# First loop of a fused transformer layer: every shift vector as a VectorE dot product, scale and shift weights in their own buffers, the first token tile in halves, a sixth pair of split weights

## The chip, the core and the metric

The kernel runs on one core of a Trainium2 chip. The engines named here are TensorE (PE in the profile, its weight loads PEld), VectorE (DVE), ScalarE (ACT), GpSimd (POOL) and SyncE (SP), whose queue issues the loads from device memory. The metric is the device time of one launch in microseconds (us); smaller is better.

## The reference

One layer over 512 latent tokens and 256 context tokens of width 1024: a half-step SwiGLU feed-forward block, a token-mixing block (latent attention beside a chunked gating MLP), and a second feed-forward block, each with a modulated RMS norm ahead of it. The change concerns the first norm and the first feed-forward weights only:

```python
mx = jnp.split((jax.nn.silu(c) @ w_ada + b_ada)[:, None, :], N_MOD, axis=-1)
mc = jnp.split((jax.nn.silu(c_ctx) @ w_ada + b_ada)[None, None, :], N_MOD, axis=-1)
...
def modulate(h, shift, scale):
    return h * (1 + scale) + shift
def ffn_sublayer(h_in, shift, scale, gate, norm_w, w1, w3, w2):
    h = modulate(rms_norm(h_in, norm_w), shift, scale)
    return h_in + 0.5 * gate * swiglu(h, w1, w3, w2)
x = ffn_sublayer(x, mx[0], mx[1], mx[2], norm1_w, ffn1_w1, ffn1_w3, ffn1_w2)
ctx = ffn_sublayer(ctx, mc[0], mc[1], mc[2], norm1_w, ffn1_w1, ffn1_w3, ffn1_w2)
```

`mx` belongs to the latent tokens, `mc` to the context tokens. Shift and scale of the first block are 2 x 1024 numbers each, and each of them is a dot product of 1024 terms with a column of `w_ada`.

## The kernel before, in words

Features lie on the 128 partitions, tokens along the free axis. The width of 1024 is cut into 8 tiles `k`; `x` holds 8 x 768 numbers per partition, two groups of 256 latent and 128 context tokens each. Every matrix product is made exact enough by splitting both operands into a high and a low part (`hh`/`hl` for activations, the `oph`/`opl` pair for weights) and adding three matmuls: high x high, high x low, low x high (`mm3`, and `first_mm` in the first loop). A pair comes from `st.pair()`; there are `OPS` = 5 of them, reused in turn. Making a pair is one ScalarE copy (`oph`) and one VectorE subtraction (`opl`).

All VectorE, ScalarE and GpSimd instructions of the part looked at here are kept in the order in which the program text has them (`nc.ordered`), and so are the TensorE instructions passed to `pin`. A helper records them, so nearly all VectorE and ScalarE rows have line 60. Loads on SP are placed by the scheduler of the framework, in the order in which it finds them ready.

**Start (lines 253 to 507).** `x` is loaded in four pieces, then the weights of the first tiles. ScalarE and VectorE square `x` (`square0`, 4 buffers, tag `sqx0`); TensorE sums the squares over the partitions by a matmul with `ones` (line 487) into `sumx`; `rstd_start` and `rstd_end` turn the sum into 1/rms by a table root on ScalarE (`r`) and one Newton step of three VectorE instructions (`v`). TensorE also multiplies `sc` (silu of the two conditioning vectors) by the identity, which spreads it over all partitions in `cb`.

**First loop (lines 530 to 575),** over `k`. It multiplies the 8 tiles of the normed latent tokens by the weights of the first two feed-forward tiles (`NFIRST` = 2, two matrices each, so 4 PSUM banks `pbs`), and makes the operands of the next tile meanwhile:

- *Scale and shift of tile k+2.* `ada_row` multiplies `sc` by the weights on TensorE (line 318); the result is a row of 2 x 128 numbers, which `ada_copy` (ScalarE) copies and `ada_col` (line 330) turns into a column by a tiny matmul; a ScalarE instruction makes the factor `a` from it. The shift comes either out of the same row (tiles in `ROWS2` = 1, 2, 3, whose row has 256 columns) or, for the other tiles, from two VectorE dot products over 1024 numbers (`ada_dot`, output `junk`, one for latent, one for context tokens), which `ada_shift` issues.
- *Operands of tile k+1.* `first_x` (VectorE, output `hfull`) is x times `a` times 1/rms; `first_h` (ScalarE, `hh`) adds the shift `s` and rounds to the high part; `first_l` (VectorE, `hl`) makes the low part.
- *Matmuls of tile k* (line 525), 12 of 512 columns: `first_mm` for 2 of the 4 banks, then the column of tile k+1, the row of tile k+2, and the other 2 banks.
- *Context tokens.* Their squares (ScalarE) and the sum of the squares (VectorE) come at k = 1 and 2, the sum over partitions at k = 3 (line 538, placed ahead of the column of tile 4), then their normed tiles two at a time, and their matmuls (`first_ctx`, line 518, 24 of 256 columns for two tiles) from k = 4 on.

One load of 1 MB (`block`) brings the scale and the shift weights of a tile, one of 256 KB (`raw`, three buffers) its feed-forward weights. Behind the loop, further feed-forward tiles follow on TensorE in a fixed order (lines 940 to 984).

Of the kernel before, what the change touches and what calls it, by code (L numbers as in the profile page):

```python
# [9 lines left out]
F32 = mybir.dt.float32  # L10
# [3 lines left out]
ALU = mybir.AluOpType  # L14
# [18 lines left out]
NFIRST = 2  # L33
ROWS2 = (1, 2, 3)
W1 = 2 * NFIRST * P
# [139 lines left out]
def layer_kernel(ctx: ExitStack, tc: tile.TileContext, xT, wfirst, wst, wada, wuq, wkpe, cols, wrope, vnw, rope, out):  # L175
# [80 lines left out]
    load_x = lambda k, n, c: nc.sync.dma_start(four(x[:, k : k + n, :], c), four(xT[:, k : k + n, :], c))  # L256
    for k in range(0, NK, 2):
        load_x(k, 2, slice(0, 256))

    def first_units(k):  # L260
        r, rw = st.block(wada, k, sp if k % 3 == 2 else None), st.raw()
        nc.sync.dma_start(rw[:, :W1], wfirst[k])
        return r, rw

    u0, rw0 = st.raw_pool.tile([P, 2048], F32, tag="block", bufs=BLOCKS, name="block_first"), st.raw()
    nc.sync.dma_start(u0[:, :D], wada[0][:, :D])
    nc.sync.dma_start(u0[:, D:], wada[0][:, D:])
    nc.sync.dma_start(rw0[:, :W1], wfirst[0])
    units = [(u0, rw0), first_units(1)]
    units.append(first_units(2))  # L270
    for k in range(0, NK, 4):
# [41 lines left out]

    def ada_row(r, d, kts=range(NK)):
        n = 2 * P if d in ROWS2 else P
        o = pa[0:2, :n]
        for kt in kts:
            pin(nc.tensor.matmul(o, sc[:, kt, :], r[:, kt * n : kt * n + n], start=kt == 0, stop=kt == NK - 1))
        return o

    def ada_copy(o, d):
        n = o.shape[1]
        row = sp.tile([2, 2 * P], F32, tag="row", name=f"row_{d}")[:, :n]
        nc.scalar.copy(row, o)
        return row

    def ada_col(row, d):
        o = [pcol[:, 4 * d + 2 * i : 4 * d + 2 * i + 2] for i in range(2)]
        for i in range(2 if d in ROWS2 else 1):
            pin(nc.tensor.matmul(o[i], row[:, i * P : i * P + P], ident[0:2, 0:2], start=True, stop=True))  # L330
        nc.scalar.activation(
            pairs[0][1][:, d, :], o[0], AF.Identity, bias=b1n[:, d : d + 1], scale=col[:, COL_N1 + d : COL_N1 + d + 1])
        if d in ROWS2:
            nc.scalar.activation(pairs[0][0][:, d, :], o[1], AF.Identity, bias=col[:, d : d + 1])

    def ada_shift(r, d, alone=False):
        for which in range(2) if d not in ROWS2 else ():
            ada_dot(r[:, D:], d, which, accs[:, d, which : which + 1])
            if alone:
                nc.scalar.activation(mod_s[0][which][:, d : d + 1], accs[:, d, which : which + 1], AF.Identity, bias=col[:, d : d + 1])  # L340
            yield
        if not alone and d not in ROWS2:
            nc.scalar.activation(pairs[0][0][:, d, :], accs[:, d, :], AF.Identity, bias=col[:, d : d + 1])

# [93 lines left out]

    def square0(which, k, on_vector=False):
        sel, n, _ = parts[which]  # L440
        sq = sp.tile([P, n], F32, tag=f"sqx{which}", bufs=4 if which == 0 else NK, name=f"sq0_{which}{k}")
        if on_vector:
            nc.vector.tensor_mul(two(sq), sel(x, k), sel(x, k))
        else:
            nc.scalar.activation(two(sq), sel(x, k), AF.Square)
        return sq

    def rstd_start(which, pt):
        n = parts[which][1]
        t = lambda s: sp.tile([P, n], F32, bufs=1, name=f"{s}{which}")  # L450
        r0, v = t("r0"), t("v")
        nc.scalar.activation(r0, pt, AF.Abs_reciprocal_sqrt, bias=epsc, scale=1.0 / D)
        return pt, r0, v

    def rstd_end(pt, r0, v):
# [3 lines left out]
        return v  # L459

    def first_x(k, which):
        sel = parts[which][0]
        nc.vector.scalar_tensor_tensor(sel(hf, k), sel(x, k), mod_a[0][which][:, k : k + 1], two(rs[which]), ALU.mult, ALU.mult)

    def first_h(k, which):
        sel = parts[which][0]
        nc.scalar.activation(sel(hh, k), sel(hf, k), AF.Identity, bias=mod_s[0][which][:, k : k + 1])

    def first_l(k, which):
        sel = parts[which][0]  # L470
        nc.vector.scalar_tensor_tensor(
            sel(hl, k), sel(hf, k), mod_s[0][which][:, k : k + 1], sel(hh, k).bitcast(F32), ALU.add, ALU.subtract)
# [9 lines left out]
    put_cb = lambda w: nc.scalar.copy(cb[:, w, :], bb[w].rearrange("p g c -> p (g c)"))  # L482
    for k in range(0, NK, 2):
        sa = square0(0, k)
        sb = square0(0, k + 1, k in (2, 6))
        nc.vector.tensor_add(sa, sa, sb)
        pin(nc.tensor.matmul(sumx, ones, sa, start=k == 0, stop=k == NK - 2))
# [3 lines left out]
    r0 = rstd_start(0, sumx)  # L491
    row = ada_copy(ada_row(units[0][0], 0), 0)
    shift = ada_shift(units[0][0], 0, True)
    next(shift)
    rs = [rstd_end(*r0)]
    ada_col(row, 0)
    ops = {}

    first_x(0, 0)
    ops[0] = st.operand(units[0][1][:, :W1])  # L500
    first_h(0, 0)
    first_l(0, 0)
    ada_row(units[1][0], 1, range(4))
    put_cb(1)
    for _ in shift:
        pass
    pbs = bigs(4)
    pcs = []

    def first_ctx(k):  # L510
        for i in range(2 * NFIRST):
# [5 lines left out]
            for m, (l, r) in enumerate(((uh, rhs[0]), (uh, rhs[1]), (ul, rhs[0]))):  # L517
                pin(nc.tensor.matmul(o, l[:, c], r, start=k == 0 and m == 0 and w == 0, stop=k == NK - 1 and m == 2,
                                     skip_group_check=True))

    def first_mm(k, i):
        uh, ul = ops[k]
        c = slice(i * P, i * P + P)
        for m, (l, r) in enumerate(((uh, hh), (uh, hl), (ul, hh))):
            pin(nc.tensor.matmul(two(pbs[i]), l[:, c], lat(r, k), start=k == 0 and m == 0, stop=k == NK - 1 and m == 2))

    ctx_h = {3: (0, 1), 4: (2, 3), 5: (4, 5), 6: (6, 7)}
    sqx = {1: 4, 2: 8}
    sqs = []
    for k in range(NK):  # L530
        if k + 3 < NK:
            units.append(first_units(k + 3))
        later = k + 2 < NK
        for i in range(NFIRST):
            first_mm(k, i)
        if k == 3:
            sumx = mm()[:, :256]
            pin(nc.tensor.matmul(sumx, ones, sqs[0], start=True, stop=True))
        if k == 0:
            row = ada_copy(ada_row(units[1][0], 1, range(4, NK)), 1)  # L540
            first_mm(0, NFIRST)
        if k + 1 < NK:
            ada_col(row, k + 1)
        if later:
            o = ada_row(units[k + 2][0], k + 2)
        for i in range(NFIRST + (k == 0), 2 * NFIRST):
            first_mm(k, i)
        shift = ada_shift(units[k + 2][0], k + 2) if later else iter(())
        next(shift, None)
        if k + 1 < NK:  # L550
            first_x(k + 1, 0)
            ops[k + 1] = st.operand(units[k + 1][1][:, :W1])
            first_h(k + 1, 0)
            next(shift, None)
            first_l(k + 1, 0)
        if later:
            row = ada_copy(o, k + 2)
        next(shift, None)
        if k == 3:
            rs.append(rstd_end(*rstd_start(1, sumx)))  # L560
# [6 lines left out]
        for j in ctx_h.get(k - 1, ()):  # L567
            first_ctx(j)
        if k in sqx:
            while len(sqs) < sqx[k]:  # L570
                sqs.append(square0(1, len(sqs)))
                if len(sqs) > 1:
                    nc.vector.tensor_add(sqs[0], sqs[0], sqs[-1])
        if k == 5:
            nc.scalar.activation(epsc2, epsc, AF.Silu)
# [1273 lines left out]
```

## Time and profile before

| | |
|---|---|
| runs | 1157.81, 1159.8, 1160.19 us (median 1159.8) |
| profiled execution | 1158.67 us, its span 1156.8 us |
| TensorE busy over the span | 1138.6 us (98%) |
| VectorE busy | 904.1 us (78%) |
| ScalarE busy | 532.1 us (46%) |
| TensorE clock granted | 1.000 |

The span runs from the first to the last instruction; the time of the execution also holds what lies around it. A row of the timeline gives start, length, engine, line, operation, what it writes and reads, how many instructions it stands for, and in brackets how long the engine was idle before it and what ended that. Busy times of TensorE rows overlap, since matmuls are pipelined: the distance from one start to the next tells the cost, not the length. The first matmul of line 525 starts at 18.58 us, and the loop's last ones end at about 77 us.

### The profile page before, as it was taken

What the parts mean: (1) busy time and instruction counts of PE and PEld (TensorE: products, weight loads), DVE (VectorE), ACT (ScalarE), POOL (GpSimd) and SP (SyncE); (2) the same over time, 40 slices, a digit from 0 to 9 for tenths busy, and PEclk for the clock granted to TensorE, in tenths of its full rate; (3) what the DMA queues carried; (4) which work ended last, traced back from release to release, by engine and by line L of the source; (5) the groups of instructions that cost most, each with busy time, mean ns of one, the idle gap of its engine ahead of it and who ended that gap; (6) DMA issues with size and microseconds to landing.
All of it is one profiled execution on the core that took longest, in us unless ns stands there. A gap on an engine that the chain in (4) does not pass through costs nothing. (4 is left out here: it accounts for less than half of the span.)

```text
span 1156.8 us, 18703 instructions
## 1 busy us (share of the span) xinstructions
PE 1138.6 (98%) x7070; PEld 1070.8 (93%) x7070; DVE 904.1 (78%) x1670; ACT 532.1 (46%) x1075; POOL 321.1 (28%) x277
## 2 busy tenths in 40 slices
PE   9999999999999999999999999999999999999998
PEld 5699999999999999999988788999999989898997
DVE  4777989888888778867746969869876859686884
ACT  4454431441344213444745549876543535353441
POOL 0001402320433013300017636670013425152330
PEclk9999999999999999999999999999999999999999
DMA  9441244334334664312242111002221322333312
GB/s 341 148 150 37 92 146 145 111 142 153 107 128 146 218 207 166 138 60 72 83 146 91 56 37 56 20 1 76 72 92 55 130 89 75 109 110 110 110 37 92
DMA packets 34650, 125.89 MB, mean 109 GB/s; under 512 B 3584, under 2 KB 10496, under 8 KB 29056
## 3 DMA queue, kind: packets, MB, share of 16 engines
q1 hardware_dynamic: 34416, 124.63, 31.4%
q8 instruction: 56, 0.92, 0.3%
q14 instruction: 34, 0.28, 0.1%
q10 hardware_dynamic: 144, 0.06, 0.0%
HBM read 122.58 MB, written 2.10 MB: 108 GB/s over the span
## 5 line engine op out<-in xcount | busy, mean ns | idle before, releaser
L60 POOL TENSOR_TENSOR block<-block 128x512 f32<-128x512 f32 x69 | 104.7, 1518 | 392.5 <-DVE opl L60 389.8
L60 DVE TENSOR_TENSOR opl<-block,oph 128x512 fp32r<-128x512 f32 x216 | 184.1, 859 | 31.3 <-ACT oph L60 29.2
L60 ACT CAST oph<-block 128x512 fp32r<-128x512 f32 x216 | 133.8, 621 | 144.1 <-PE mm L60 92.4
L60 PE MATMUL mm<-gh,oph 128*128 128x384 f32 (+1 forms) x440 | 155.2, 353 | 0.0
L60 PE MATMUL mm<-gl,oph 128*128 128x384 f32 (+1 forms) x440 | 154.9, 352 | 0.0
L60 PE MATMUL mm<-gh,opl 128*128 128x384 f32 (+1 forms) x440 | 154.9, 352 | 0.0
L60 DVE SCALAR_TENSOR_TENSOR x<-mm,g,x 128x256 f32<-128x256 f32 (+2 forms) x184 | 82.8, 489 | 47.8 <-PE mm L60 47.1
L60 ACT CAST oph<-raw 128x512 fp32r<-128x512 f32 x106 | 64.4, 620 | 92.6 <-PE mm L60 68.4
L60 POOL TENSOR_TENSOR block<-s,block 128x512 f32<-128x512 f32 x35 | 48.6, 1389 | 158.7 <-DVE opl L60 158.0
L60 PEld LDWEIGHTS mm<-gh,opl 128*128 128x128 f32 x440 | 82.6, 188 | 5.7
L60 PEld LDWEIGHTS mm<-gh,oph 128*128 128x128 f32 x440 | 82.6, 188 | 5.6
L60 PEld LDWEIGHTS mm<-gl,oph 128*128 128x128 f32 x440 | 82.6, 188 | 5.6
L60 DVE TENSOR_TENSOR opl<-raw,oph 128x512 fp32r<-128x512 f32 x106 | 71.0, 684 | 9.3 <-ACT oph L60 8.8
L60 PE MATMUL mm<-hh,oph 128*128 128x384 f32 x192 | 64.6, 336 | 0.0
L60 PE MATMUL mm<-hl,oph 128*128 128x384 f32 x192 | 64.2, 334 | 0.0
L60 PE MATMUL mm<-hh,opl 128*128 128x384 f32 x192 | 64.1, 334 | 0.0
L60 DVE SCALAR_TENSOR_TENSOR junk<-raw,cb 128x1024 bf16<-128x1024 f32 x48 | 63.3, 1332 | 0.4 <-DMA raw<-wada 0.4
L60 POOL TENSOR_TENSOR s<-block 128x512 f32<-128x512 f32 x34 | 50.6, 1489 | 19.6 <-DMA block<-wst 19.6
L60 PE MATMUL one<-hh,oph 128*128 128x384 f32 x144 | 48.1, 334 | 0.0
L60 PE MATMUL one<-hl,oph 128*128 128x384 f32 x144 | 48.1, 334 | 0.0
L60 PE MATMUL one<-hh,opl 128*128 128x384 f32 x144 | 48.1, 334 | 0.0
L60 DVE SCALAR_TENSOR_TENSOR raw<-raw,cb 128x1024 f32<-128x1024 f32 x32 | 41.0, 1288 | 9.0 <-DMA raw<-wada 9.0
(649 smaller groups left out, 3464.6 us busy)
## 6 DMA issues: line engine op xcount, KB each, us to landing
raw<-wst SPq DMA_DIRECT2D x77, 512.0 KB, 3.7
block<-wst SPq DMA_DIRECT2D x36, 1024.0 KB, 4.9
raw<-wada SPq DMA_DIRECT2D x56, 512.0 KB, 4.2
block<-wada SPq DMA_DIRECT2D x7, 1024.0 KB, 6.2
x<-xT SPq DMA_DIRECT2D x6, 512.0 KB, 6.8
raw<-wfirst SPq DMA_DIRECT2D x8, 256.0 KB, 4.7
out<-x SPq DMA_DIRECT2D x7, 256.0 KB, 2.5
block_first<-wada SPq DMA_DIRECT2D x2, 512.0 KB, 8.2
```

What stands on the lines that cost most here:

```text
L60: return lambda *a, **k: self.tc.keep_in_program_order(f(*a, **k))
```

## The change

It does five things. (1) `ROWS2` goes: every row has 128 columns, and all 16 shift values (8 tiles, latent and context) are VectorE dot products, each followed by a small ScalarE instruction of its own. The latent one of tile k+2 is issued in iteration k, the context one of tile k in iteration k. (2) Scale weights have three buffers of 512 KB (`sa`), shift weights share a 1 MB block two tiles at a time; `x` comes in five pieces. (3) 1/rms is made in two halves of 256 tokens, and so is the first tile: `first_half` runs 12 matmuls of 256 columns for each half. (4) A sixth pair of split weights takes two of the `sqx0` buffers (tile 5); in the first four tiles `oph` moves to the head of the iteration and `opl` ahead of `first_x`, in the later ones both come behind. (5) The squares of the context tokens are all added in iteration 2, and their sum over partitions moves behind the column of tile 4. The reordering of the weights on the host goes with (1).

```diff
-ROWS2 = (1, 2, 3)
-    for k in range(0, NK, 2):
-        load_x(k, 2, slice(0, 256))
+    for k, n in ((0, 2), (2, 2), (4, 2), (6, 1), (7, 1)):
+        load_x(k, n, slice(0, 256))
     def first_units(k):
-        r, rw = st.block(wada, k, sp if k % 3 == 2 else None), st.raw()
+        ra = sp.tile([P, D], F32, tag="sa", bufs=3, name=f"scale_{k}")
+        nc.sync.dma_start(ra, wada[k][:, :D])
+        if k % 2 == 0:
+            sblk.append(st.raw_pool.tile([P, 2048], F32, tag="block", bufs=BLOCKS, name=f"shift_{k}"))
+        rs_ = sblk[-1][:, (k % 2) * D : (k % 2) * D + D]
+        nc.sync.dma_start(rs_, wada[k][:, D:])
+        rw = st.raw()
         nc.sync.dma_start(rw[:, :W1], wfirst[k])
...
+    def ada_shift(d, which):
+        ada_dot(units[d][1], d, which, accs[:, d, which : which + 1])
+        nc.scalar.activation(mod_s[0][which][:, d : d + 1], accs[:, d, which : which + 1], AF.Identity, bias=col[:, d : d + 1])
...
-    for k in range(0, NK, 2):
+    for k in (0, 2):
         sa = square0(0, k)
-        sb = square0(0, k + 1, k in (2, 6))
+        sb = square0(0, k + 1)
         nc.vector.tensor_add(sa, sa, sb)
-        pin(nc.tensor.matmul(sumx, ones, sa, start=k == 0, stop=k == NK - 2))
+        sums(sumx, sa, k == 0, False)
     put_cb(0)
+    sq = [square0(0, k) for k in (4, 5, 6)]
+    nc.vector.tensor_add(sq[0], sq[0], sq[1])
+    nc.vector.tensor_add(sq[0], sq[0], sq[2])
     nc.vector.tensor_scalar_add(b1, col[:, COL_B : COL_B + 72], 1.0)
+    sq[1] = square0(0, 7)
+    put_cb(1)
...
+    for i in range(2):
+        sums(sumx, sq[i], False, i == 1, 0)
+    rstd_root(*rl, half_of(0))
+    ada_row(0)
+    row = ada_copy(0)
+    for i in range(2):
+        sums(sumx, sq[i], False, i == 1, 1)
     ada_col(row, 0)
+    oph(0)
+    rstd_steps(*rl, half_of(0))
+    rstd_root(*rl, half_of(1))
+    ada_shift(0, 0)
+    first_x(0, 0, 0)
+    first_h(0, 0, 0)
+    opl(0)
+    first_l(0, 0, 0)
+    rstd_steps(*rl, half_of(1))
+    first_x(0, 0, 1)
+    first_h(0, 0, 1)
...
+        if n < OPS - 1:
+            oph(n)
+        if k == 0:
+            first_half(0)
+            ada_row(1)
+            row = ada_copy(1)
+            ada_shift(1, 0)
+            first_l(0, 0, 1)
+            first_half(1)
+            ada_col(row, 1)
+        else:
+            for i in range(NFIRST):
+                first_mm(k, i)
+            if n < NK:
+                ada_col(row, n)
         if k == 3:
-            sumx = mm()[:, :256]
-            pin(nc.tensor.matmul(sumx, ones, sqs[0], start=True, stop=True))
+            sumc = mm()
+            sums(sumc, sqs[0], True, True)
+        if k + 2 < NK:
+            ada_row(k + 2)
+        if k:
+            for i in range(NFIRST, 2 * NFIRST):
+                first_mm(k, i)
+        for j in ctx_h.get(k - 1, ()):
+            first_ctx(j)
+        if n < NK:
+            ada_shift(k, 1)
+            if k == 6:
+                ada_shift(7, 1)
+            if n < OPS - 1:
+                opl(n)
+            first_x(n, 0)
+            first_h(n, 0)
+            if k + 2 < NK:
+                row = ada_copy(k + 2)
+            if n >= OPS - 1:
+                oph(n)
+            if k + 2 < NK:
+                ada_shift(k + 2, 0)
+            first_l(n, 0)
+            if n >= OPS - 1:
+                opl(n)
+        if k in (1, 2):
+            for j in range(4 * k - 4, 4 * k):
+                sqs.append(square0(1, j))
+        if k == 2:
+            for sq_ in sqs[1:]:
+                nc.vector.tensor_add(sqs[0], sqs[0], sq_)
```

More of the change, by code (lines that the diff above doesn't have):

```diff
@@ L256, in layer_kernel @@
     load_x = lambda k, n, c: nc.sync.dma_start(four(x[:, k : k + n, :], c), four(xT[:, k : k + n, :], c))
-    for k in range(0, NK, 2):
-        load_x(k, 2, slice(0, 256))
+    for k, n in ((0, 2), (2, 2), (4, 2), (6, 1), (7, 1)):
+        load_x(k, n, slice(0, 256))
+    sblk, units = [], []
     def first_units(k):
-        r, rw = st.block(wada, k, sp if k % 3 == 2 else None), st.raw()
-        nc.sync.dma_start(rw[:, :W1], wfirst[k])
[L263 to L270, printed above, removed]
+        ra = sp.tile([P, D], F32, tag="sa", bufs=3, name=f"scale_{k}")
[5 more added lines that the diff above has]
+        rw = st.raw()
+        nc.sync.dma_start(rw[:, :W1], wfirst[k])
+        units.append((ra, rs_, rw[:, :W1]))
+    for k in range(3):
+        first_units(k)
     for k in range(0, NK, 4):
@@ L312, in mod_final, with ada_row, ada_copy @@
                 nc.vector.tensor_scalar_mul(mod_g[i][which][:, cs], mod_g[i][which][:, cs], 0.5)
[L314 to L324, printed above, removed]
+    def ada_row(d):
+        for kt in range(NK):
+            pin(nc.tensor.matmul(pa[0:2, :P], sc[:, kt, :], units[d][0][:, kt * P : kt * P + P], start=kt == 0, stop=kt == NK - 1))
+    def ada_copy(d):
+        row = sp.tile([2, P], F32, tag="row", name=f"row_{d}")
+        nc.scalar.copy(row, pa[0:2, :P])
         return row
     def ada_col(row, d):
-        o = [pcol[:, 4 * d + 2 * i : 4 * d + 2 * i + 2] for i in range(2)]
-        for i in range(2 if d in ROWS2 else 1):
-            pin(nc.tensor.matmul(o[i], row[:, i * P : i * P + P], ident[0:2, 0:2], start=True, stop=True))
+        o = pcol[:, 2 * d : 2 * d + 2]
+        pin(nc.tensor.matmul(o, row, ident[0:2, 0:2], start=True, stop=True))
         nc.scalar.activation(
[L332 to L343, printed above, removed]
+            pairs[0][1][:, d, :], o, AF.Identity, bias=b1n[:, d : d + 1], scale=col[:, COL_N1 + d : COL_N1 + d + 1])
+    def ada_shift(d, which):
+        ada_dot(units[d][1], d, which, accs[:, d, which : which + 1])
+        nc.scalar.activation(mod_s[0][which][:, d : d + 1], accs[:, d, which : which + 1], AF.Identity, bias=col[:, d : d + 1])
     def ada_rest():
@@ L446, in square0, with sums, rstd_tiles, rstd_root @@
         return sq
-    def rstd_start(which, pt):
+    def sums(dst, sq, first, last, g=None):
+        c = slice(0, sq.shape[1]) if g is None else slice(256 * g, 256 * g + 256)
+        pin(nc.tensor.matmul(dst[:, c], ones, sq[:, c], start=first, stop=last, skip_group_check=True))
+    def rstd_tiles(which):
         n = parts[which][1]
[L450 to L455, printed above, removed]
+        return [sp.tile([P, n], F32, bufs=1, name=f"{s}{which}") for s in ("r0", "v")]
+    def rstd_root(pt, r0, v, c):
+        nc.scalar.activation(r0[:, c], pt[:, c], AF.Abs_reciprocal_sqrt, bias=epsc, scale=1.0 / D)
+    def rstd_steps(pt, r0, v, c):
+        pt, r0, v = pt[:, c], r0[:, c], v[:, c]
         nc.vector.scalar_tensor_tensor(v, pt, EPS * D, r0, ALU.add, ALU.mult)
@@ L458, in rstd_end, with sel_of, first_x, first_h @@
         nc.vector.scalar_tensor_tensor(v, v, 1.5, r0, ALU.add, ALU.mult)
[L459 to L466, printed above, removed]
+    def sel_of(which, g):
+        f = parts[which][0]
+        return f if g is None else lambda t, k: f(t, k)[:, g]
+    def first_x(k, which, g=None):
+        sel = sel_of(which, g)
+        r = two(rs[which])
+        nc.vector.scalar_tensor_tensor(
+            sel(hf, k), sel(x, k), mod_a[0][which][:, k : k + 1], r if g is None else r[:, g], ALU.mult, ALU.mult)
+    def first_h(k, which, g=None):
+        sel = sel_of(which, g)
         nc.scalar.activation(sel(hh, k), sel(hf, k), AF.Identity, bias=mod_s[0][which][:, k : k + 1])
-    def first_l(k, which):
-        sel = parts[which][0]
+    def first_l(k, which, g=None):
+        sel = sel_of(which, g)
         nc.vector.scalar_tensor_tensor(
@@ L482, in layer_kernel, with oph, opl @@
     put_cb = lambda w: nc.scalar.copy(cb[:, w, :], bb[w].rearrange("p g c -> p (g c)"))
-    for k in range(0, NK, 2):
+    for k in (0, 2):
         sa = square0(0, k)
-        sb = square0(0, k + 1, k in (2, 6))
+        sb = square0(0, k + 1)
         nc.vector.tensor_add(sa, sa, sb)
-        pin(nc.tensor.matmul(sumx, ones, sa, start=k == 0, stop=k == NK - 2))
+        sums(sumx, sa, k == 0, False)
     put_cb(0)
+    sq = [square0(0, k) for k in (4, 5, 6)]
+    nc.vector.tensor_add(sq[0], sq[0], sq[1])
+    nc.vector.tensor_add(sq[0], sq[0], sq[2])
     nc.vector.tensor_scalar_add(b1, col[:, COL_B : COL_B + 72], 1.0)
+    sq[1] = square0(0, 7)
+    put_cb(1)
     nc.vector.tensor_mul(b1n, b1[:, NK : 2 * NK], col[:, COL_N1 : COL_N1 + NK])
[L491 to L495, printed above, removed]
-    ada_col(row, 0)
[L497 to L506, printed above, removed]
+    ops = {}
+    def oph(k):
+        ops[k] = st.pair() if k != OPS else [sp.tile([P, 512], F32R, tag="sqx0", bufs=4, name=f"op5{p}") for p in "hl"]
+        nc.scalar.copy(ops[k][0], units[k][2])
+    def opl(k):
+        nc.vector.tensor_sub(ops[k][1], units[k][2], ops[k][0].bitcast(F32))
+    rl = [sumx, *rstd_tiles(0)]
+    rs = [rl[2]]
+    half_of = lambda g: slice(256 * g, 256 * g + 256)
+    for i in range(2):
[5 more added lines that the diff above has]
+        sums(sumx, sq[i], False, i == 1, 1)
+    ada_col(row, 0)
+    oph(0)
[9 more added lines that the diff above has]
+    first_h(0, 0, 1)
     pbs = bigs(4)
@@ L519, in first_ctx, with first_half @@
                                      skip_group_check=True))
+    def first_half(g):
+        uh, ul = ops[0]
+        for m, (l, r) in enumerate(((uh, hh), (uh, hl), (ul, hh))):
+            for i in range(2 * NFIRST):
+                pin(nc.tensor.matmul(two(pbs[i])[:, g], l[:, i * P : i * P + P], lat(r, 0)[:, g], start=m == 0 and g == 0, stop=False,
+                                     skip_group_check=True))
     def first_mm(k, i):
@@ L524, in first_mm @@
         for m, (l, r) in enumerate(((uh, hh), (uh, hl), (ul, hh))):
-            pin(nc.tensor.matmul(two(pbs[i]), l[:, c], lat(r, k), start=k == 0 and m == 0, stop=k == NK - 1 and m == 2))
+            pin(nc.tensor.matmul(two(pbs[i]), l[:, c], lat(r, k), start=False, stop=k == NK - 1 and m == 2, skip_group_check=True))
     ctx_h = {3: (0, 1), 4: (2, 3), 5: (4, 5), 6: (6, 7)}
-    sqx = {1: 4, 2: 8}
     sqs = []
     for k in range(NK):
+        n = k + 1
         if k + 3 < NK:
[L532 to L535, printed above, removed]
-        if k == 3:
-            sumx = mm()[:, :256]
[L538 to L558, printed above, removed]
@@ L566, in layer_kernel @@
             first_l(j, 1)
[L567 to L573, printed above, removed]
         if k == 5:
@@ L1808 @@
     first = np.concatenate([t[:, :, 1].transpose(2, 1, 0, 3).reshape(NK, P, 1024), t[:, :, 0].transpose(2, 3, 0, 1).reshape(NK, P, 1024)], 2)
-    rows2 = np.stack([t[:, :, 1], t[:, :, 0]], 3).transpose(2, 1, 0, 3, 4).reshape(NK, P, 2048)
-    first[list(ROWS2)] = rows2[list(ROWS2)]
     rest = t[:, :, 2:].transpose(2, 3, 4, 0, 1).reshape(28, 2, P, D).transpose(0, 2, 1, 3).reshape(28, P, 2048)
```

14 lines of the change are left out of this document (11 added, 3 removed).

## The prediction

> **What bounds the kernel now.** I read the busy shares first, then the busy time of the stretches of the first loop, then its timeline.
>
> ```profile
> PE 1138.6 (98%) x7070; PEld 1070.8 (93%) x7070; DVE 904.1 (78%) x1670; ACT 532.1 (46%) x1075; POOL 321.1 (28%) x277
> ```
> ```profile
> 29.80:36.80 7.00, 7.00 (x33) 3.96 (x32) 3.70 (x7) 3.34 (x9) 0.00 (x0) 1.00 0.64 234
> ...
> 49.10:58.80 9.70, 8.28 (x55) 6.64 (x54) 7.29 (x15) 3.74 (x9) 0.00 (x0) 1.00 0.19 60
> ...
> sum 58.50, PE 56.13 PEld 40.06 DVE 40.41 ACT 26.69 POOL 0.00; mean PE 7.02 PEld 5.01 DVE 5.05 ACT 3.34 POOL 0.00
> ```
>
> Columns: stretch, length, busy us of PE, PEld, DVE, ACT, POOL, granted clock, DMA share, GB/s. TensorE is busy for all but 2.4 of the loop's 58.5 us, VectorE idle for 18.1. So TensorE's order sets the loop's end, and VectorE has room, most of it in the iterations with wide rows (3.70 of 7.00). Only in the sixth iteration does TensorE wait for long.
>
> ```profile
> 23.97 3.62 PE L318 MATMUL mm<-block,sc 128*2 128x256 f32 x16
> 27.52 0.50 PE L525 MATMUL big<-hh,oph 128*128 128x512 f32 x1
> 29.79 0.60 PE L330 MATMUL mm<-ident,row 2*128 2x2 f32 x4
> ...
> 43.08 0.70 PE L538 MATMUL mm<-sq,ones 128*128 128x256 f32 x2 [0.59 <-DVE sq L60]
> 43.71 0.38 PE L330 MATMUL mm<-ident,row 2*128 2x2 f32 x2
> ...
> 52.73 0.28 PE L518 MATMUL mm<-hh,oph 128*128 128x256 f32 x1
> 54.24 0.62 ACT L60 CAST oph<-raw 128x512 fp32r<-128x512 f32 x1 [3.47 <-PE mm L518]
> 55.60 0.43 PE L525 MATMUL big<-hh,oph 128*128 128x512 f32 x1
> 57.45 0.50 PE L525 MATMUL big<-hl,oph 128*128 128x512 f32 x1 [1.42 <-DVE hl L60]
> 58.80 0.38 PE L330 MATMUL mm<-ident,row 2*128 2x2 f32 x2
> 59.11 1.91 PE L318 MATMUL mm<-block,sc 128*2 128x128 f32 x16
> 60.95 0.50 PE L525 MATMUL big<-hh,oph 128*128 128x512 f32 x1
> 66.79 0.38 PE L330 MATMUL mm<-ident,row 2*128 2x2 f32 x2
> 77.08 0.34 PE L60 MATMUL mm<-hh,oph 128*128 128x384 f32 x1
> ```
>
> A wide row costs TensorE 27.52 - 23.97 = 3.55 us, a narrow one 60.95 - 59.11 = 1.84. The wait at 57.45 starts with ScalarE: the copy for tile 5 needs the pair of tile 0, which the context matmuls (52.73 to 55.60: 24 in 2.87 us) still read. A whole iteration, column to column, is 66.79 - 58.80 = 7.99, so without context matmuls 5.12. The loop hands over at 77.08.
>
> **Part 1, narrow rows: what TensorE is spared.** Three rows fall by 1.71 us, 5.1 in all. The double column takes 0.60 (at 29.79) where the single one takes 0.38 (at 58.80): about 0.2 each, 0.6 in all; the single one delays the next row by 59.11 - 58.80 = 0.31. With the wait of tile 5 (57.45 instead of 0.23 after 55.60: 1.6) some 7.3 us could go. What follows is what comes back.
>
> **Part 2, the price on VectorE.**
>
> ```profile
> 41.01 2.02 DVE L60 TENSOR_TENSOR sq<-sq,sq 128x256 f32<-128x256 f32 x4
> 42.94 1.22 DVE L60 SCALAR_TENSOR_TENSOR junk<-block,cb 128x1024 bf16<-128x1024 f32 x1
> ...
> 47.73 0.42 DVE L60 SCALAR_TENSOR_TENSOR v<-mm,r 128x256 f32<-128x256 f32 x1
> ...
> 50.97 1.22 DVE L60 SCALAR_TENSOR_TENSOR junk<-block,cb 128x1024 bf16<-128x1024 f32 x1
> 52.12 0.75 DVE L60 SCALAR_TENSOR_TENSOR hfull<-x,a,v 128x512 f32<-128x512 f32 x1
> ...
> 67.21 0.35 ACT L60 ACTIVATE a<-mm,b1n,col 128x2 f32<-128x2 f32 x1 [0.88 <-PE mm L330]
> 67.59 0.75 DVE L60 SCALAR_TENSOR_TENSOR hfull<-x,a,v 128x512 f32<-128x512 f32 x1 [2.26 <-ACT a L60]
> 68.26 0.68 DVE L60 TENSOR_TENSOR opl<-raw,oph 128x512 fp32r<-128x512 f32 x1
> 68.38 0.72 ACT L60 ACTIVATE hh<-hfull,s 128x512 fp32r<-128x512 f32 x1 [0.31 <-DVE hfull L60]
> 69.14 0.75 DVE L60 SCALAR_TENSOR_TENSOR hl<-hfull,s,hh 128x512 fp32r<-128x512 f32 x1 [0.19 <-ACT hh L60]
> 69.80 0.88 DVE L60 SCALAR_TENSOR_TENSOR hfull<-x,a,v 128x256 f32<-128x256 f32 x2
> ...
> 71.66 0.68 DVE L60 TENSOR_TENSOR s<-block 128x512 f32<-128x512 f32 x1
> ```
>
> A dot takes 52.12 - 50.97 = 1.15 us of VectorE, `first_x` 0.67, `first_l` the same, `opl` about 0.62, an addition of context squares (42.94 - 41.01) / 4 = 0.48. Six dots more are 6.9 us. An ordinary iteration is then 2 x 1.15 + 2 x 0.67 + 0.62 = 4.3 us of VectorE against 5.12 of TensorE, and one with two context tiles 4.3 + 4 x 0.44 (half of 69.80's 0.88) = 6.1 against 7.99: hidden. The order within an iteration matters more. From the start of the column, `first_x` comes at +0.80 (67.59 - 66.79), then a dot, then `first_l` at +2.6, seen by TensorE 0.8 later (0.78 from 17.80 to 18.58 in the rows of part 3, for the high part; taken the same here): +3.4. TensorE, after column, row and 6 matmuls of 0.23, wants the high part at 0.31 + 1.84 + 1.38 = +3.5 and the low part at +3.8. It fits by 0.4, so that cover is thin; were it gone, each ordinary iteration would pay the excess.
>
> It is gone in two places. In iteration 2 seven additions (3.4 us) stand behind `first_l` of tile 3 and end at column + 6.65; the sum over partitions, now behind column 4, is reached at 5.12 + 0.31, so TensorE waits 1.3, then spends 43.71 - 43.08 = 0.63. What is late next, `first_x` of tile 4 and then of tile 5 behind the context's Newton steps (1.3), is caught up: tile 5 starts 2.4 late, but 2.87 of context matmuls stand ahead of its use. The other place is the start.
>
> **Part 3, the start in halves.**
>
> ```profile
> 10.72 0.69 DVE L60 TENSOR_TENSOR sq<-x 128x512 f32<-128x512 f32 x1
> ...
> 12.14 0.69 DVE L60 TENSOR_TENSOR sq<-sq,sq 128x512 f32<-128x512 f32 x1 [0.73 <-ACT sq L60]
> ...
> 12.88 0.30 PEld L487 LDWEIGHTS mm<-sq,ones 128*128 128x128 f32 x2 [0.56 <-DVE sq L60]
> ...
> 13.94 1.91 PE L318 MATMUL mm<-block_first,sc 128*2 128x128 f32 x16
> 14.05 0.69 ACT L60 ACTIVATE r<-mm,epsc 128x512 f32<-128x512 f32 x1 [1.05 <-PE mm L487]
> ...
> 17.02 0.75 DVE L60 SCALAR_TENSOR_TENSOR hfull<-x,a,v 128x512 f32<-128x512 f32 x1
> ...
> 17.80 0.72 ACT L60 ACTIVATE hh<-hfull,s 128x512 fp32r<-128x512 f32 x1 [0.33 <-DVE hfull L60]
> ...
> 18.58 0.50 PE L525 MATMUL big<-hh,oph 128*128 128x512 f32 x1 [0.19 <-ACT hh L60]
> ```
>
> The last squares take about as long as now: square 6 where one stands at 10.72, its addition to 12.1, half a square to 12.7. The last sum over 512 columns needs 13.94 - 12.88 = 1.06, over 256 half: row 0 starts at 13.3 (not before; at the latest at 13.94 as now, if square 6 finds no free buffer). Then row 0 (1.84), then the second half's sums, 4 passes of 0.22, to 16.0, seen at 16.3. The Newton steps of the first half stand behind these sums in the program and read the same PSUM tile. Either they wait (16.3), or they follow the first root (14.0), and then the column of tile 0 (16.1, `first_x` at 16.95) is last. No row here decides between them; I take 16.3, since the tile is one bank being written, and keep the other end, 1.3 us earlier.
>
> [...]
>
> From 16.3: three half steps 1.3 (0.44 each, from 47.73's row), a dot 1.15, half an `first_x`, half an `hh`: first matmul at 19.85, 1.3 later than now. VectorE goes on with `opl`, low part (to 20.25), three steps, half an `first_x`, a dot (23.1), the low part of the second half, seen at 23.7. TensorE: 12 matmuls at 0.12 (as line 518), row 1, 12 more, behind that low part, to 24.7: column 1 at 24.85. Then `first_x` 25.65, a dot, `first_l` 27.5, seen at 28.3, while TensorE is through row 2 at 27.0: about 1.0 lost. Five matmuls later column 2 starts at 29.5, against 29.79. The start gives back nearly all that row 2 saves.
>
> **The loads.** The shift of tile 4 shares its block with tiles 0 and 1, and can be loaded only after VectorE's second dot of tile 1 (29.3).
>
> ```profile
> raw<-wada SPq DMA_DIRECT2D x56, 512.0 KB, 4.2
> ```
>
> At 4.2 us from issue it lands near 34, and its dot comes at 35.9. Tile 6's waits for the dot at 43.4, lands by 48, and is wanted at 50.4. SP's queue behind it holds weights wanted later still. I cost this at nothing, 2 us if a landing takes 6.
>
> **The sum.** Column 2 at 29.5; columns 3 and 4 at +5.12 each: 34.6 and 39.7 (now 43.71). Column 5: 5.12 + 1.3 + 0.63 = 46.8. Columns 6 and 7: 7.99 each: 54.8, 62.8 (now 66.79). From there 77.08 - 66.79 = 10.29 as now: 73.1, which is 4.0 us sooner. Behind it TensorE is without gaps for long:
>
> ```profile
> 120.00:130.00 10.00, 10.00 (x58) 9.50 (x57) 9.49 (x16) 4.24 (x8) 2.33 (x3) 1.00 0.32 106
> ```
>
> so an earlier start carries through. The profiled execution of 1158.67 (span 1156.8) becomes 1154.7; the median of the runs stands 1.1 above it: 1155.8. The bounds: halves that overlap, -1.3; row 0 at 13.94, +0.6; dots at their full row, 1.22 + 0.08, in the five that lie on the path, +0.8. Own range 1154.3 to 1157.4, with some room for the runs.
>
> **Rivals.** *The halves overlap:* gain 5.3, 1154.5; for it, the root of the first half is free at 14; against it, the program's order and the shared tile. *VectorE hands the gain back behind the loop:* it is 9.49 of 10 us busy at 120 to 130. Its first later instruction moves from 71.66 to 68.4 only (column 7 at 62.8, `first_x` 0.80 on, `first_l` 69.14 - 67.59 = 1.55 on, then 0.67, `opl` 0.62 and 1.96 for the context), 3.3 sooner; with dots at 1.30, 16 x 0.15 = 2.4 of that is lost as well, leaving 0.9: 1158.9. Against it: TensorE does not idle in that stretch, so VectorE has slack. *VectorE becomes the bound, slower than before:* at full row lengths its work from 16.3 is 20.8 (16 dots), 12.4 (latent x and low parts), 5.5 (`opl`), 3.0 (additions), 3.9 (Newton steps), 7.0 (context), together 52.6, so it ends at 68.9 and the last context matmuls at 71.8 if it never idles. It decides from 5.3 us of idle time, for each further one is lost. Half of today's 18.1 would give 80.9, 3.8 later than 77.08: 1163.6. For it: every `first_x` waits for ScalarE's `a`; against it: the dot of the next tile fills those waits. That the sixth pair does nothing I rule out: its buffers are the squares', long free by tile 5.
>
> **How the numbers follow.** The forecast 0.60, overlapping halves 0.10, handed back 0.16, VectorE the bound 0.14. About 0.2% (2.3 us) is what a measurement of this kernel can tell from no change. Faster takes the first two and a little of the third, 0.73; same the rest of the third and a sliver of the last, 0.15; slower 0.12. The range for 8 in 10 runs from 1153.0 (overlap and a quick run) to 1159.4, which takes in the handed-back case.
>
> **What would show it.** Right: line 318 has only 128-column rows; column 4 near 39.7; no ScalarE wait for line 518 ahead of `oph` of tile 5; a wait of about 1.3 at the context's sum; the first later matmul near 73. The start: Newton steps at 16.3 or at 14, first matmul at 19.85 or 18.6. Wrong: TensorE waiting for `hl` in every iteration, VectorE idle for `a` while TensorE stands, a dot waiting for a load, or a handover at 73 and the old time at the end.

## The result, and the profile after

The changed kernel takes 1159.64 us (median of 14 executions, 1156.93 to 1161.6) against 1159.31 (14 executions, 1157.14 to 1160.19): ratio 1.0001, 95% interval 0.9991 to 1.0011. That is no change; 1155.8 was forecast. Its profiled execution takes 1157.04 us, with a span of 1155.2.

The page of the changed kernel, its busy times (compare the prediction's first fence):

```profile
PE 1134.3 (98%) x7080; PEld 1072.5 (93%) x7080; DVE 909.6 (79%) x1687; ACT 534.1 (46%) x1085; POOL 320.3 (28%) x277
```

TensorE is 4.3 us less busy and VectorE 5.5 us more, in the direction that the spared rows and the added dots had to bring; and yet the end hardly moves. Two stretches show where the time went. These are the windows of the changed kernel (stretch, length, busy us of PE, PEld, DVE, ACT, POOL, then the granted clock, DMA share, GB/s):

```profile
15.30:18.65 3.35, 0.01 (x1) 0.00 (x1) 3.25 (x8) 2.04 (x5) 0.00 (x0) 1.00 1.02 391
18.65:19.57 0.92, 0.92 (x7) 0.92 (x8) 0.89 (x3) 0.00 (x0) 0.00 (x0) 1.00 1.19 309
19.57:22.98 3.41, 3.41 (x18) 2.33 (x18) 3.34 (x7) 1.02 (x2) 0.00 (x0) 0.50 1.16 324
22.98:40.73 17.75, 17.05 (x105) 12.32 (x103) 14.08 (x25) 9.18 (x27) 0.00 (x0) 1.00 0.79 272
40.73:42.44 1.71, 0.00 (x0) 0.00 (x0) 1.33 (x4) 0.35 (x1) 0.00 (x0) 1.00 0.02 5
42.44:46.87 4.43, 4.43 (x20) 2.60 (x21) 3.57 (x6) 1.54 (x4) 0.00 (x0) 0.62 0.47 125
46.87:75.77 28.90, 28.90 (x188) 24.65 (x187) 25.59 (x48) 15.61 (x36) 0.00 (x0) 1.00 0.45 154
```

TensorE stands still for 3.35 us before its first half tile, and for 1.71 us before the sum of the context squares. After each of the two, the clock granted to it is halved for 3.41 us: 0.50 from 19.57 to 22.98, and again from 43.46 to 46.87, which the row from 42.44 on shows as a mean of 0.62 over 4.43 us. Before had no such stretch in its profile; the mean granted clock there was 1.000, here 0.997.

The timeline of the changed kernel at the same places (start, length, engine, line, operation, what it writes and reads; line 549 is the half tile, 556 the whole tile, 444 the sum over partitions, 318 the row, 327 the column):

```profile
3.51 0.22 ACT L279 ACTIVATE sc<-col 128x16 f32<-128x16 f32 x1 [0.84 <-DMA col<-cols]
...
3.87 4.78 PE L483 MATMUL big<-ident,sc 128*128 128x128 f32 x32
...
12.14 0.47 ACT L59 ACTIVATE r<-mm,epsc 128x256 f32<-128x256 f32 x1 [0.75 <-PE mm L444]
13.87 1.13 PE L444 MATMUL mm<-sq,ones 128*128 128x256 f32 x4
15.11 0.42 DVE L59 SCALAR_TENSOR_TENSOR v<-mm,r 128x256 f32<-128x256 f32 x1 [3.69 <-PE mm L444]
18.65 0.74 PE L549 MATMUL big<-hh,oph 128*128 128x256 f32 x4 [3.34 <-ACT hh L59]
20.88 2.92 PE L318 MATMUL mm<-scale,sc 128*2 128x128 f32 x16
23.73 0.74 PE L549 MATMUL big<-hh,oph 128*128 128x256 f32 x4
30.15 0.38 PE L327 MATMUL mm<-ident,row 2*128 2x2 f32 x2
...
40.35 0.38 PE L327 MATMUL mm<-ident,row 2*128 2x2 f32 x2
42.44 0.70 PE L444 MATMUL mm<-sq,ones 128*128 128x256 f32 x2 [1.71 <-DVE sq L59]
43.07 3.24 PE L318 MATMUL mm<-scale,sc 128*2 128x128 f32 x16
46.24 0.78 PE L556 MATMUL big<-hh,oph 128*128 128x512 f32 x1
49.49 0.38 PE L327 MATMUL mm<-ident,row 2*128 2x2 f32 x2
75.77 0.34 PE L59 MATMUL mm<-hh,oph 128*128 128x384 f32 x1
```

Row 1 takes 23.73 - 20.88 = 2.85 us and row 5 takes 46.24 - 43.07 = 3.17, where a narrow row cost 1.84 in the profile of before. The handover at 75.77 looks 1.3 us earlier than before's 77.08, but this execution as a whole starts sooner, because its first small load (`col`) lands sooner: ScalarE's `sc` waits for it until 3.51, in before until 4.30, and TensorE's first spread matmul waits for `sc`. The same two of before:

```profile
4.30 0.21 ACT L277 ACTIVATE sc<-col 128x16 f32<-128x16 f32 x1 [1.61 <-DMA col<-cols]
...
4.67 5.91 PE L479 MATMUL big<-ident,sc 128*128 128x128 f32 x32 [0.70 <-ACT sc L277]
```

Counted from the spread matmul, the handover comes at 77.08 - 4.67 = 72.4 before and at 75.77 - 3.87 = 71.9 after: 0.5 us gained, of 4.0 forecast. It can be less: a second profile of the kernel before (`before_again`, below) has these rows:

```profile
4.21 5.05 PE L479 MATMUL big<-ident,sc 128*128 128x128 f32 x32 [0.25 <-ACT sc L277]
...
76.19 0.34 PE L60 MATMUL mm<-hh,oph 128*128 128x384 f32 x1
```

That is 76.19 - 4.21 = 72.0, only 0.1 more than after. The same spread matmuls take 5.05 us here and 5.91 in the first profile, and from their start to the first matmul of line 525 it is 0.4 us less. So the gain up to the handover is 0.1 to 0.5 us, depending on which execution of before it is counted against.

### The profile page after: what moved, and what is told of

It is laid out like the page before. It is cut to its first block, busy times and chain, and to the rows that moved or that the text cites. A ratio compares the mean times of both kernels' runs of the same rounds, so it can differ in the third digit from the quotient of the medians.

```text
span 1155.2 us, 18757 instructions
## 1 busy us (share of the span) xinstructions
PE 1134.3 (98%) x7080; PEld 1072.5 (93%) x7080; DVE 909.6 (79%) x1687; ACT 534.1 (46%) x1085; POOL 320.3 (28%) x277
```

## The experiments

Theory G: what TensorE is spared is lost to the halved clock that the two new waits bring. Rivals: VectorE's dots cost what TensorE is spared, whatever the clock (V); the waits count only by their length (W, C); the clock was halved as often before (R). All executions count, with the mean of their granted clocks:

| kernel | executions | median us | ratio to before, 95% interval | mean clock |
|---|---|---|---|---|
| changed kernel | 14 | 1159.64 | 1.0001 (0.9991 to 1.0011) | 0.9957 |
| before, again (before_again) | 11 | 1159.10 | 1.0003 (0.9994 to 1.0012) | 0.9993 |
| idle products at the start (warm_start) | 12 | 1157.34 | 0.9985 (0.9973 to 0.9998) | 0.9987 |
| idle products at both waits (warm_both) | 8 | 1156.24 | 0.9975 (0.9965 to 0.9985) | 0.9991 |
| row 1 into the first wait (row1_early) | 9 | 1156.14 | 0.9975 (0.9962 to 0.9988) | 0.9992 |
| sum behind the matmuls (sum_late) | 12 | 1157.11 | 0.9985 (0.9975 to 0.9996) | 0.9973 |
| both moves (row1_sum) | 11 | 1156.11 | 0.9972 (0.9963 to 0.9981) | 0.9992 |
| before, a wait opened (gap_before) | 8 | 1162.06 | 1.0026 (1.0016 to 1.0036) | 0.9982 |
| before, two rows narrow (narrow_two) | 11 | 1157.31 | 0.9983 (0.9974 to 0.9991) | 0.9993 |
| before, three rows narrow (narrow_three) | 10 | 1155.23 | 0.9972 (0.9963 to 0.9981) | 0.9994 |
| the last, with the sixth pair (narrow_pair) | 6 | 1155.08 | 0.9969 (0.9958 to 0.9981) | 0.9988 |
| the last, two things later (narrow_late) | 10 | 1155.11 | 0.9968 (0.9957 to 0.9979) | 0.9988 |

The kernel before, measured beside them on the same chips, has medians of 1159.29, 1158.97 and 1158.49 us.

**The clock of before.** No edit.

> The kernel before, unchanged, to see the granted TensorE clock of its executions. Theory G (the gain is lost to the halved clock): the executions of before show a clock of 1.000 or close to it, so that they lose less to it than those of the changed kernel (0.997 and 0.994). Rival R (the clock is halved as often before, and the gain is lost elsewhere): its executions show 0.997 and 0.994 as often as the changed kernel's. Time by both: 1159.3 us, within 1.5.

Ten of its 11 executions show 0.999 or 1.000 and one 0.998; the changed kernel has 0.997 in eight (1156.93 to 1159.89 us) and 0.994 in six (1160.02 to 1161.6). R falls. The mean differs by 0.0036, which over 1157 us is 4.2 us of full clock more that is missing (an estimate from the two means): about as much as was forecast as gain.

**Idle products in the waits.** Nothing is taken out of the changed kernel; products of a matrix of ones, which nobody reads, are put into the waits.

```diff
     ada_col(row, 0)
+    for _ in range(7):
+        pin(nc.tensor.matmul(two(warm[:, :256]), ones, ones2, start=True, stop=True))
     oph(0)
```

> The changed kernel with 7 idle products of ones (14 passes of 256 columns, some 3.0 us) into an unused PSUM tile, in the 3.3 us in which TensorE waits for the first half tile. Theory G: the stretch of half clock at 19.6 to 23.0 us is gone from the profile, the first loop hands over about 1.3 us sooner (74.4 instead of 75.8), the clock in its executions rises by 0.0015, and the median falls by 1 to 2 us. Rival R: clock and time stay as in the changed kernel, or the added products delay the first matmul and the time rises.

```diff
             sumc = mm()
+            for _ in range(4):
+                pin(nc.tensor.matmul(two(sumc[:, 256:512]), ones, ones2, start=True, stop=True, skip_group_check=True))
             sums(sumc, sqs[0], True, True)
```

> As the last, and 4 idle products more (8 passes, some 1.7 us) ahead of the sum of the context squares, where TensorE waits 1.7 us. Theory G: both stretches of half clock are gone, the clock is 1.000 in most executions, the handover comes about 2.7 us sooner than in the changed kernel (near 73.1, the forecast), and the median falls to 1155.5 to 1157. Rival R: no change beyond 0.5 us.

The first gives 1157.34 us, the second 1156.24. By the ratios to before that is 0.16% and 0.26%, or 1.8 and 3.0 us, less than the changed kernel, by work that is of no use; the second's interval (up to 0.9985) lies clear of the changed kernel's (from 0.9991). The timeline of the kernel with both:

```profile
16.79 3.29 PE L521 MATMUL mm<-ones 128*128 128x256 f32 x14
20.20 0.74 PE L551 MATMUL big<-hh,oph 128*128 128x256 f32 x4
...
40.31 0.38 PE L327 MATMUL mm<-ident,row 2*128 2x2 f32 x2
40.62 1.99 PE L584 MATMUL mm<-ones 128*128 128x256 f32 x8
42.45 0.64 PE L444 MATMUL mm<-sq,ones 128*128 128x256 f32 x2
43.02 1.91 PE L318 MATMUL mm<-scale,sc 128*2 128x128 f32 x16
44.86 0.50 PE L558 MATMUL big<-hh,oph 128*128 128x512 f32 x1
```

The idle products end where the waits ended, and row 5 is back at 44.86 - 43.02 = 1.84 us. W falls: TensorE's own work waits as long as in the changed kernel (the sum starts 42.45 - 40.31 = 2.14 us behind the column of tile 4, there 42.44 - 40.35 = 2.09). The clock in the first of the two was expected 0.0015 up and rose 0.0030; its profile has no half clock behind the first wait, but has it behind the second, from 41.71 to 45.12, after a wait of 1.80 us. With both waits filled, three of the eight executions show 1.000, where most were expected to.

**The two moves.** Useful work goes into the waits instead.

```diff
     first_h(0, 0, 1)
+    ada_row(1)
     pbs = bigs(4)
...
             first_half(0)
-            ada_row(1)
```

> The changed kernel with the row of tile 1 alone moved ahead of the first half tile's matmuls; the sum of the context squares stays where it is. Theory G: the half clock at 20 to 23 us is gone, the one at 43 to 47 us stays in most executions, the clock lies at 0.997 to 0.998 where the changed kernel has 0.994 to 0.997, and the median is 1156.5 to 1158. Rival W (only the waits themselves count, not the clock): the gain over the changed kernel (1159.6) is at most the 1.8 us of the row.

```diff
-        if k == 3:
-            sumc = mm()
-            sums(sumc, sqs[0], True, True)
         if k + 2 < NK:
             ada_row(k + 2)
         if k:
             for i in range(NFIRST, 2 * NFIRST):
                 first_mm(k, i)
+        if k == 3:
+            sumc = mm()
+            sums(sumc, sqs[0], True, True)
```

> The changed kernel with the sum of the context squares alone moved behind the last six matmuls of tile 3; the row of tile 1 stays between the halves. Theory G: the second stretch of half clock is gone and the first stays, clock 0.997 to 0.999, median 1157 to 1158.5: the 1.7 us wait and the 1.4 us that the second stretch took. Rival W: at most the 1.7 us of the wait, 1157.9 or above, at the clock of the changed kernel.

> The changed kernel with two products moved and nothing added: the row of tile 1 goes ahead of the first half tile's matmuls, into the 3.3 us wait, and the sum of the context squares goes behind the last six matmuls of tile 3. Theory G: the waits are filled with work that is needed, so that no stretch of half clock is left in the loop, the clock is 0.999 to 1.000, and the median is 1154 to 1156 us, below that of the kernel with idle products at both places (1156.2). Rival V (VectorE is the bound once the clock is right): the clock is full, but the median stays above 1156.2.

Row 1 alone gives 0.26%, or 3.0 us, which is more than the 1.8 us of the row, though the intervals alone would not exclude 1.8; the clock, 0.9992 against 0.9957, speaks for G. But my picture of the second wait was too simple: with the first wait filled, the clock is 0.998 to 1.000, not the 0.997 to 0.998 I expected, although TensorE still waits 1.7 us for the sum. The profile of that kernel shows the wait and a row at full speed behind it:

```profile
40.41 0.70 PE L444 MATMUL mm<-sq,ones 128*128 128x256 f32 x2 [1.72 <-DVE sq L59]
41.04 1.91 PE L318 MATMUL mm<-scale,sc 128*2 128x128 f32 x16
42.88 0.50 PE L557 MATMUL big<-hh,oph 128*128 128x512 f32 x1
```

So a wait of 1.7 us was followed by half clock in two profiles (1.71 us in the changed kernel's, 1.80 in that of `warm_start`) and not in this one (1.72; what they differ in is taken up at the end). All 14 executions of the changed kernel have a mean clock of 0.997 or less, which is what its profile shows with both stretches; where the slow stretches of the other 13 lay is not on record. Moving the sum alone gives 0.16%, or 1.8 us, which W's 1.7 would cover as well; there the start is left as it was, its profile has the clock low for longer, and its executions stay at 0.995 to 0.999. These are its windows (the clock stands third from the end):

```profile
15.00:20.00 5.00, 1.66 (x9) 1.57 (x9) 4.83 (x11) 2.04 (x5) 0.00 (x0) 0.77 1.07 371
20.00:25.00 5.00, 5.00 (x25) 3.29 (x25) 4.03 (x8) 1.17 (x3) 0.00 (x0) 0.55 1.10 350
25.00:30.00 5.00, 4.31 (x32) 3.21 (x32) 2.83 (x5) 2.55 (x8) 0.00 (x0) 1.00 0.59 193
```

With both moves the median is 1156.11, no better than row 1 alone (1156.14) and slightly above the 1154 to 1156 I expected.

**A wait opened in the kernel before.** Half of row 1, which stood in the wait for the first tile, goes to its other half behind six matmuls.

```diff
-    ada_row(units[1][0], 1, range(4))
...
-            row = ada_copy(ada_row(units[1][0], 1, range(4, NK)), 1)
+            row = ada_copy(ada_row(units[1][0], 1), 1)
```

> The kernel before with the half of row 1 that stands in the wait for the first tile moved behind the first six matmuls, to the other half; same instructions, same count. Theory G: TensorE now waits some 2.1 us at one piece before its first matmul, in part of the executions the clock is halved for 3.4 us, and the median rises by the 1.9 us that are no longer hidden and by up to 1.5 more, to 1161 to 1163, with a clock below before's (0.998 and less in the slower ones). Rival C (a wait of this length does not touch the clock): 1161.2 at an unchanged clock.

1162.06 us against 1158.97 beside it, 3.1 more, with the same instructions; the clock is 0.997 to 0.999 in its eight executions, never 1.000. Its timeline:

```profile
18.34 0.50 PE L524 MATMUL big<-hh,oph 128*128 128x512 f32 x1 [2.00 <-ACT hh L60]
19.12 0.79 PE L524 MATMUL big<-hl,oph 128*128 128x512 f32 x1 [0.28 <-DVE hl L60]
19.71 0.63 PE L524 MATMUL big<-hh,opl 128*128 128x512 f32 x1
20.14 0.63 PE L524 MATMUL big<-hh,oph 128*128 128x512 f32 x1
20.57 0.63 PE L524 MATMUL big<-hl,oph 128*128 128x512 f32 x1
```

After 2.00 us of waiting, matmuls start 0.43 us apart instead of the 0.23 they take in the prediction's rows. So half clock behind a wait shows without any part of the change: 1.9 us is work that is no longer hidden (half a wide row, 1.89 us in the profile of before), and the other 1.2 fits a clock that the trace has at one half from 18.74 to 22.16, which can take at most half of those 3.41 us, 1.7 (an estimate). C falls, since the clock did change.

**Parts of the change on the kernel before.** The start and the order of before stay; only rows become narrow. For two rows the set of wide rows shrinks to tile 1; for three, tile 1's dots are added behind tile 0's.

```diff
-ROWS2 = (1, 2, 3)
+ROWS2 = ()
...
     for _ in shift:
         pass
+    for _ in ada_shift(units[1][0], 1):
+        pass
```

> The kernel before with narrow rows and VectorE dots for tiles 2 and 3 alone (two of the three wide rows; nothing else of the change). Theory G: TensorE is spared 2 x 1.9 = 3.8 us of rows; with no new wait the median falls by 2.5 to 3.8 us, unless a clock below 1.000 shows that the spared time was lost to it. Rival V (VectorE's dots cost what TensorE is spared, clock or not): the gain is under 1 us at a clock of 1.000.

> The kernel before with all three narrow rows, the two dots of tile 1 placed behind the dots of tile 0, and nothing else of the change; half of row 1 stays in the wait at the start. Theory G: another 1.9 us of row 2 is spared, no new wait comes, the clock is as in before, and the median falls to 1155 to 1156.5. Rival V: at a full clock the median stays at that of two narrow rows (1157.3) or above.

```diff
-            ops[k + 1] = st.operand(units[k + 1][1][:, :W1])
+            src = units[k + 1][1][:, :W1]
+            ops[k + 1] = st.operand(src) if k + 1 != OPS else st.split(
+                [sp.tile([P, 512], F32R, tag="sqx0", bufs=4, name=f"op5{p}") for p in "hl"], src)
```

> As the last, with the sixth pair of split weights out of the squares' buffers for tile 5. Theory: the 1.7 us wait of TensorE for the low part of tile 5 goes, and the median falls by 1 to 1.7 us more, to 1153.5 to 1155.5. Rival: the wait goes, but VectorE's two dots stand in its place, and the median does not move by more than 0.5.

Two narrow rows give 2.0 us (1157.31 against 1159.29), below the 2.5 to 3.8 expected; three give 3.7 (1155.23 against 1158.97; 3.2 by the ratio), at before's clock. V, by which less than 1 us would come, falls. But the dots are not wholly hidden in this order: TensorE's waits for low parts in the first loop, 1.7 us in the profile of `before_again`, are 3.0 in that of two narrow rows, and this 1.3 is most of what is missing from the 3.8 us that TensorE is spared there. The sixth pair brought 0.15 us in the median, where 1 to 1.7 was expected; the interval doesn't tell that from nothing. Its wait did go: by the profiles, TensorE's waits for low parts fall from 3.0 to 1.6 us, and the iteration of tile 5 takes 54.99 - 47.00 = 7.99 us from column to column instead of 55.53 - 45.82 = 9.71. But that profile has half clock from 18.63 to 22.04, and its column 2 is 0.8 us late. Its six executions have a lower mean clock (0.9988 against 0.9994). Whether that took the gain in the other five as well stays open.

Last, the sum is moved here too, and the context dot of tile 1 to the end of the first iteration:

```diff
-    for _ in ada_shift(units[1][0], 1):
-        pass
+    shift1 = ada_shift(units[1][0], 1, True)
+    next(shift1)
...
+        if k == 3:
+            sumx = mm()[:, :256]
+            pin(nc.tensor.matmul(sumx, ones, sqs[0], start=True, stop=True))
         shift = ada_shift(units[k + 2][0], k + 2) if later else iter(())
...
+        if k == 0:
+            for _ in shift1:
+                pass
         if k == 3:
```

> The kernel before with three narrow rows and the sixth pair (1155.1), the context dot of tile 1 put behind the first iteration's other work, and the sum of the context squares behind the last six matmuls of tile 3. Theory: of the waits that are left there (1.0 us for the high part of tile 1, 0.6 for the sum, 1.6 for low parts) about 1.5 us go, and the median is 1153.5 to 1155. Rival: VectorE is as long as TensorE by then, and the median stays at 1155.

1155.11 us, the median of the last kernel. The waits only changed place, as TensorE's list of waits in its first loop shows (total us, times, longest):

```profile
PE big L527 <- DVE hl L60: 2.6, 5, 0.7
PE big L527 <- ACT hh L60: 0.9, 1, 0.9
PE mm L318 <- DMA block<-wada: 0.6, 1, 0.6
```

The three kernels near 1155.1 beat before, and so the changed kernel, by some 3 to 4 us; they can't be told apart.

## Why the prediction was wrong

**The step that failed** is in parts 2 and 3: a wait of TensorE was costed at its length. Part 3 put the first matmul at 19.85 with nothing on TensorE since the column of tile 0, and part 2 left a wait of 1.3 us at the context's sum; that the clock would be halved for 3.41 us behind each was in no term, no bound and no rival. The runs showed 3.5 us in its place, nearly all of the forecast gain.

**The terms, each counted from the first spread matmul** (4.67 before, 3.87 after). The first half tile: forecast 19.85 - 4.67 = 15.2, measured 14.8. Column 2: forecast 24.8, measured 26.3, so 1.4 late, all of it behind 19.57, where the clock falls. Columns 3 and 4 come 5.1 us apart as forecast (40.35 is 1.4 late still). Column 5: forecast 42.1, measured 45.6, 2.1 later again: row 5 took 1.33 too long, the sum waited 1.71 instead of 1.3, and the matmuls at the end of the slow stretch make up the rest. From column 5 to the handover the forecast was 73.1 - 46.8 = 26.3, measured 75.77 - 49.49 = 26.3. So 3.5 of the 4.0 us went in those two places. About 0.4 of it is the longer wait; the rest is the clock, for two stretches of 3.41 us at 0.50 can take up to 3.4 (an estimate). The profiled execution is one of the eight at 0.997; in the six at 0.994 the clock was low for about twice as long (an estimate from the two means).

**What held.** The narrow rows and the six dots cost what the rows said, and in the changed order VectorE hid them: TensorE waits for a low part only once, for 0.6 us, ahead of column 2. The wait for the pair of tile 0 is gone, and the time behind the handover is the same: 1156.8 - 77.08 = 1079.7 us before, 1155.2 - 75.77 = 1079.4 after, so what is gained in the loop does carry through. The choice between 16.3 and 14.0 for the Newton steps fell on the right side: the first half's root is out at 12.61, and the step starts at 15.11, after the second half's sums (the 3.69 us wait), which end at 15.00. The prediction chose 16.3 because the tile is one bank being written; the trace shows the wait and what ended it, and no run shows that the bank is the reason. No dot waited for a load.

**The rivals.** The halves did not overlap. VectorE did not hand the gain back, nor did it become the bound: with TensorE kept busy by products of no use, and VectorE's order as it is, the time falls to 1156.24, 0.4 from the forecast; by the ratio, 3.0 of the 4.0 us are back. The result of "no change" came by a road that none of them named.

**The chances.** No change had 0.15, as the tail of the rival that hands the gain back. The mean granted clock of 1.000 in before's profile stood there to be read, and so did the half row that keeps TensorE busy in the wait for the first tile; the prediction did not ask what it was there for.

## What to carry to other kernels

When a change makes TensorE wait where it worked before, cost the wait at its length plus what a halved clock can take from the work behind it (here up to 1.7 us for each stretch of 3.41 at 0.50, an estimate), and look at the granted clock of all executions, not of one: a wait of 1.7 to 1.8 us was followed by half clock in two profiles and not in a third (last section). Put needed work into a wait rather than behind it, even if it is no earlier needed there: moving one row of 1.84 us gained some 3 us. Where a bundle moves the time by nothing, run its parts on the old order: narrow rows alone gave 3.2 to 3.7 of the 4.0 us that were forecast for the whole.

## What the runs showed of the hardware

A wait of 2.00 us was followed by matmuls 0.43 us apart instead of 0.23 in the profile of the kernel with the opened wait, and all eight of its executions had a clock below 1.000 (0.997 to 0.999). A wait of 1.7 to 1.8 us was followed by half clock in the profiles of the changed kernel (1.71) and of `warm_start` (1.80), and not in that of the kernel with row 1 moved (1.72).

What decides between them was not tried, but the traces show more than the waits' lengths. In the changed kernel's, the granted clock changes at 19.57, 22.98, 43.46 and 46.87, which are 4, 5, 11 and 12 times 3.41 us behind 5.91, where the trace's record of the clock begins. In before's the record begins at 9.07, and the clock stays full up to 1150 us. I cut both, up to there, into steps of 3.41 us from the start of the record and took the share of each in which TensorE was busy. In the changed kernel's the two lowest, 0.27 and 0.50, were followed by half clock, and the others, from 0.62 up, were not; in before's the lowest was 0.56. The second wait of the changed kernel stands in the first row below (1.70 of 3.41, 0.50), the same wait with row 1 moved in the second (1.77, 0.52), behind which the clock was full:

```profile
40.05:43.46 3.41, 1.70 (x10) 0.91 (x9) 2.69 (x7) 0.35 (x1) 0.00 (x0) 1.00 0.06 20
38.77:42.18 3.41, 1.77 (x13) 1.20 (x14) 3.10 (x7) 0.60 (x2) 0.00 (x0) 1.00 0.01 2
```

Another case lies outside the loop. The profiles of before and of the changed kernel have the same two waits, of about 0.75 and 1.33 us, near 650 us. With three narrow rows TensorE is busy for 1.61 of 3.42 us there (0.47; first two rows), and the next step is at half clock; in the profile of before one such step has 1.98 of 3.41 (0.58; last two rows), and the clock stays full:

```profile
650.19:653.61 3.42, 1.61 (x9) 1.14 (x10) 3.42 (x7) 2.82 (x5) 1.93 (x1) 1.00 0.00 0
653.61:657.02 3.41, 3.41 (x9) 2.65 (x8) 3.41 (x10) 1.38 (x2) 3.20 (x2) 0.50 0.00 0
...
654.19:657.60 3.41, 1.98 (x11) 1.40 (x12) 3.41 (x8) 2.44 (x5) 2.30 (x1) 1.00 0.00 0
657.60:661.02 3.42, 3.42 (x17) 2.82 (x16) 3.42 (x10) 1.38 (x2) 3.21 (x2) 1.00 0.00 0
```

Against these stands the profile with the sixth pair, where a step with 0.59 was followed by half clock. So the share alone does not settle it, and no run was built to test it.
